# Seven products for eight in all large projections of a two-layer decoder trunk, with the middle of the layer in another order

## The chip, the core and the metric

One Trainium2 chip, and one of its cores. The engines of the core that matter here: TensorE (PE), which multiplies matrices into PSUM; VectorE (DVE) and ScalarE (ACT), which work on tiles of 128 partitions; SyncE (SP), whose queue issues the loads. The metric is the time of one execution on the device in microseconds (us).

## What is computed

Two layers over 256 tokens (S) of 2048 channels (D), all in float32:

```python
for i in range(DEPTH):
    h = rmsnorm(x, norm_mix_g[i])
    proj = h @ w_in[i]
    glu_in, q, k, v, f_logit, g_conv, g_attn = jnp.split(proj, split_pts, axis=-1)
    y_conv = conformer_conv(glu_in, ...)          # GLU, 31 taps, LayerNorm, swish, @ w_conv_out
    y_attn = forgetting_attention(q, k, v, log_f).reshape(...) @ w_attn_out[i]
    merged = sigmoid(g_conv) * y_conv + sigmoid(g_attn) * y_attn
    x = x + merged @ w_out[i]
    hf = rmsnorm(x, norm_ffn_g[i])
    gate, up = jnp.split(hf @ w_gate_up[i], 2, axis=-1)
    x = x + (silu(gate) * up) @ w_down[i]
    hp = rmsnorm(x, norm_ple_g[i])
    x = x + sigmoid(hp @ w_ple_gate[i]) * (p[i] @ w_ple_proj[i])
return rmsnorm(x, final_g)
```

There are 8 heads of 128 channels, 1024 channels of convolution, 5632 hidden channels in the feed-forward part and 256 channels of the embeddings p.

## The kernel before, in words

**Weights.** Every weight is streamed from HBM once, in tiles `raw` of 128x1024 float32 (two k-tiles of 128 rows by 512 columns), in a pool of seven. ACT rounds a tile to `wh` (line 140) and DVE subtracts to get the remainder `wl` (line 141); there are four buffers of each. The activations are split in the same way into xh and xl. A product of a k-tile is then three matmuls of 128x512: xh by wh, xh by wl, xl by wh (lines 175 to 177, in `Sum.add`). With two row blocks of tokens, one split tile `raw` feeds 12 matmuls.

**Two ways to make an output.** `chunk` makes 512 columns for all 256 tokens in the plain way, in groups of four k-tiles. `fast_chunks` makes two chunks of 512 columns together: of the first four k-tiles, taken as two halves of K, with the two chunks as the other dimension, it forms the eight block products with seven, as in Strassen's method in Winograd's form. That takes 42 matmuls for 48, sums of weight tiles on DVE (line 241 with `raw` and `sum`), a copy on ACT (line 254) and sums of the results `u` on DVE (lines 241, 255, 256, 271, 272), and an operand `Fast`, whose eight parts come from four subtractions (line 320) and two splits (lines 329, 330). The other k-tiles of the pair (`left`) are plain. Before the change, only the gate and up products of the feed-forward part, all but the first chunk, are made so: ten pairs in a layer.

**Stages of a layer.** Input projection: two GLU pairs of chunks, values, keys and queries; then four chunks of the convolution's gate (GATE_A) and four of the attention's gate (GATE_B). wA and wC take the attention's and the convolution's outputs, wOut their sum; then gate and up (wGU) and down (wD) in three parts of 3, 4 and 4 hidden chunks; then the embeddings' product (wPP) and their gate (wPG).

**Order.** `turns`, `tasks` and `background` are queues of deferred work. `run` (after each group of four k-tiles) does one deferred turn, such as the transposes of a finished chunk (line 295), or one task of the attention: the scores of a head, the transposes of its probabilities (lines 673 to 675), or its product with v. `fill` gives the background a credit of 7 after each group: convolution taps on DVE (line 490), then the steps of the LayerNorm. A tile framework then orders the queue of each engine by the dependences and the pools; each engine runs its own queue in order.

**Norms.** `Norm.squares` sums the squares of a finished chunk of x on ACT (line 368), `turn` transposes it on PE and splits it (lines 285, 286), or, for the first chunk of a fast norm, copies it into a `Fast` (line 314). The factor 1/rms is applied later, to the products. `residual` adds an output to x (line 822).

Of the attention's softmax, line 658 masks, 663 takes the maximum, 664 is the exponential, 665 and 666 scale. Lines 725 and 731 belong to the LayerNorm. Lines 878 to 881 are the sigmoid of the embeddings' gate, its product and the addition to x.

## Time and profile before

| what | us |
|---|---|
| three runs | 2891.22, 2891.67, 2892.88 |
| the profiled execution | 2891.74 |
| its span in the trace | 2889.9 |
| DMA, mean over the span | 188 GB/s, 54% of the 16 engines' time |

The profile lists for each engine the time in which it was busy; for each group of instructions the line of the kernel, the engine, output and input, the count, the busy time, the mean of one, and the idle time of the engine just before them with what ended it. A row of the timeline gives start, length, engine, line, operation and, in brackets, how long the engine had been idle and for whom. Rows that follow each other closely stand as one row with a count (x2). A row of windows gives for a stretch the busy time and the count of PE, of its weight loads (PEld), of DVE, ACT and POOL, then the granted clock of TensorE, the DMA share and GB/s. Tiles of one kind are told without their numbers there.

### The profile page before, as it was taken

To read this page: it belongs to the slowest core of one execution; us is meant where nothing else is said; L and a number is where in the kernel's file an instruction comes from. 1 tells how busy PE (TensorE), PEld (TensorE's weight loads), DVE (VectorE), ACT (ScalarE), POOL (GpSimd) and SP (SyncE) were. 2 spreads that over 40 slices of the span, in tenths; PEclk is the share of its full clock that TensorE was granted. 3 is DMA by queue.
4 is the path that set the end of the run, shared out by engine and by line. 5 is a ranking of instruction groups with operands and counts; after the bars stand their busy time and mean duration, and the time that the engine had idled before them with its cause. 6 is when DMAs were issued, how large, how long until landed. Compare 5 with 4: busy or idle time off the path is not lost.

```text
span 2889.9 us, 34305 instructions
## 1 busy us (share of the span) xinstructions
PE 2855.0 (99%) x12884; PEld 2361.8 (82%) x12884; DVE 2001.4 (69%) x2568; ACT 1431.1 (50%) x1726; POOL 9.5 (0%) x40
## 2 busy tenths in 40 slices
PE   8999999999999999999999999999999999999998
PEld 6888888788888888888888888887888888888886
DVE  5997745557678758865569966455585886688554
ACT  5445744455445435545554456444454554455444
POOL 0000000000000000000000000000000000000000
PEclk9999999999999999999999999999999999999999
DMA  7554455455556556555555544554455555556553
GB/s 279 180 179 166 166 197 191 165 185 180 207 183 209 198 178 211 182 204 189 183 176 188 180 163 175 195 190 162 177 191 207 182 196 204 181 197 211 186 203 122
DMA packets 149496, 543.27 MB, mean 188 GB/s; under 512 B 16849, under 2 KB 17105, under 8 KB 149073
## 3 DMA queue, kind: packets, MB, share of 16 engines
q1 hardware_dynamic: 149328, 541.07, 54.1%
q8 instruction: 101, 1.65, 0.2%
q14 instruction: 67, 0.54, 0.1%
HBM read 538.91 MB, written 2.10 MB: 187 GB/s over the span
## 4 chain that ended last, share of the span: by engine, by line
PE 94%; DVE 4%; DMA 1%; ACT 0%; issue 0%; SPq 0%; POOL 0%; ACTq 0%; POOLq 0%; DVEq 0%
PE mm L176 29%; PE mm L177 29%; PE mm L175 29%; PE ms L295 2%; DVE wl L141 2%; DVE pair L490 2%; PE ms L177 2%; PE ms L176 2%; PE ms L175 2%; DMA xt<-in_xR_dram 0%; PE ms L649 0%; DMA raw<-in_wI_dram 0%; PE ms L685 0%; ACT tmp L368 0%; PE ms L651 0%
## 5 line engine op out<-in xcount | busy, mean ns | idle before, releaser
L141 DVE TENSOR_TENSOR wl<-raw,wh 128x1024 fp32r<-128x1024 f32 x1054 | 1282.3, 1223 | 802.1 <-ACT wh L140 793.8
L140 ACT ACTIVATE wh<-raw 128x1024 fp32r<-128x1024 f32 x1054 | 1116.3, 1060 | 1299.9 <-PE mm L177 1186.1
L175 PE MATMUL mm<-wh,pair 128*128 128x512 f32 x3832 | 1502.8, 392 | 18.6 <-ACT wh L140 11.1
L176 PE MATMUL mm<-wl,pair 128*128 128x512 f32 x3832 | 1495.7, 390 | 1.8 <-DVE wl L141 1.8
L177 PE MATMUL mm<-wh,pair 128*128 128x512 f32 x3832 | 1495.9, 390 | 0.0
L175 PEld LDWEIGHTS mm<-wh,pair 128*128 128x128 f32 x3832 | 721.1, 188 | 166.9 <-ACT wh L140 12.0
L176 PEld LDWEIGHTS mm<-wl,pair 128*128 128x128 f32 x3832 | 721.8, 188 | 151.7 <-DVE wl L141 3.4
L177 PEld LDWEIGHTS mm<-wh,pair 128*128 128x128 f32 x3832 | 721.4, 188 | 150.7
L490 DVE SCALAR_TENSOR_TENSOR pair<-pair,vecs,pair 128x256 f32<-128x256 f32 x480 | 201.3, 476 | 0.0
L177 PE MATMUL ms<-wh,pair 128*128 128x512 f32 x192 | 74.7, 389 | 0.0
L175 PE MATMUL ms<-wh,pair 128*128 128x512 f32 x192 | 74.7, 389 | 0.0
L176 PE MATMUL ms<-wl,pair 128*128 128x512 f32 x192 | 74.7, 389 | 0.0
L241 DVE TENSOR_TENSOR raw<-raw,raw 128x1024 f32<-128x1024 f32 x60 | 73.2, 1221 | 0.9
L283 DVE TENSOR_TENSOR pair<-ms,pair 128x512 fp32r<-128x512 f32 (+1 forms) x76 | 45.1, 625 | 1.6 <-ACT pair L282 1.3
L822 DVE TENSOR_TENSOR xt<-xt,mm 128x512 f32<-128x512 f32 x64 | 41.1, 680 | 4.9 <-PE mm L177 4.9
L175 PEld LDWEIGHTS ms<-wh,pair 128*128 128x128 f32 x192 | 36.0, 188 | 7.5
L176 PEld LDWEIGHTS ms<-wl,pair 128*128 128x128 f32 x192 | 36.0, 188 | 7.5
L177 PEld LDWEIGHTS ms<-wh,pair 128*128 128x128 f32 x192 | 36.0, 188 | 7.5
L368 ACT ACTIVATE tmp<-xt 128x512 f32<-128x512 f32 x56 | 34.6, 619 | 14.9 <-DVE xt L822 8.8
L282 ACT ACTIVATE pair<-ms 128x512 fp32r<-128x512 f32 (+1 forms) x76 | 38.0, 541 | 0.6 <-PE ms L686 0.6
L285 ACT ACTIVATE pair<-ms,vecs 128x256 fp32r<-128x256 f32 x72 | 30.6, 467 | 14.4 <-DVE pair L286 14.4
L140 ACT ACTIVATE wh<-sum 128x1024 fp32r<-128x1024 f32 x20 | 21.2, 1062 | 31.3 <-PE mm L177 31.3
(167 smaller groups left out, 925.3 us busy)
## 6 DMA issues: line engine op xcount, KB each, us to landing
raw<-in_wGU_dram SPq DMA_DIRECT2D x352, 512.0 KB, 4.1
raw<-in_wI_dram SPq DMA_DIRECT2D x287, 512.0 KB, 3.8
raw<-in_wD_dram SPq DMA_DIRECT2D x176, 512.0 KB, 3.7
raw<-in_wOut_dram SPq DMA_DIRECT2D x64, 512.0 KB, 3.7
raw<-in_wPG_dram SPq DMA_DIRECT2D x64, 512.0 KB, 3.6
raw<-in_wA_dram SPq DMA_DIRECT2D x32, 512.0 KB, 4.2
raw<-in_wC_dram SPq DMA_DIRECT2D x32, 512.0 KB, 4.3
raw<-in_wPP_dram SPq DMA_DIRECT2D x8, 512.0 KB, 3.2
```

Of the source, the lines that this page charges most:

```text
L140: act.activation(h, raw, AF.Copy)
L141: dve.tensor_tensor(l, raw, h.bitcast(F32), op=ALU.subtract)
L175: pe.matmul(self.t, lhsT=xh, rhs=wh, start=start, stop=False)
L176: pe.matmul(self.t, lhsT=xh, rhs=wl, start=False, stop=False)
L177: pe.matmul(self.t, lhsT=xl, rhs=wh, start=False, stop=self.left == 0)
L241: add = lambda o, a, b: dve.tensor_tensor(o, a, b, op=ALU.add)
L282: act.activation(hi, src, AF.Copy)
L283: dve.tensor_tensor(lo, src, hi.bitcast(F32), op=ALU.subtract)
L295: pe.transpose(pt[:, kk * S + b * P : kk * S + (b + 1) * P], src(b)[:, c : c + P], ident)
L368: act.activation(tmp(), xt[:, b, n * 512 : (n + 1) * 512], AF.Square, accum_out=self.ss[:, b * 4 + n : b * 4 + n + 1],)
L490: dve.scalar_tensor_tensor(cv[c], u[c][:, j : j + S], w, cv[c], op0=ALU.mult, op1=ALU.add,)
L822: dve.tensor_tensor(xc, xc, acc[b], op=ALU.add)
```

## The change

Seven products for eight are now used in the two gates, in the output projection, in the embeddings' gate, and in the down projection (three parts of two pairs), as well as in gate and up as before: 28 pairs more in the two layers. Norms and merged values of these stages have a `Fast` operand; that of the very first norm is made from the transposed input (`early`); that of the down projection from the first hidden chunk of its part. The buffers of a `Fast` come from another pool. `fast_chunks` hands over its first chunk as soon as that is done (`first`).

The middle of a layer has another order. Before: four GATE_A chunks, with the second half of the attention and of the LayerNorm's work beneath them; then GATE_B and wA in turns; then four wC. Now: two GATE_B pairs, then the rest of the attention's tasks, four wA; then a GATE_A pair and two wC, twice. The credit of `fill` is split into 3 and 4 for each half group. The embeddings' products of two chunks are made ahead of a wPG pair, and ACT copies them out of PSUM (line 932 of the changed kernel).

```diff
-    def fast_chunks(fast, w1, w2, xs, ks):
+    def fast_chunks(fast, w1, w2, xs, ks, first, to=None):
...
-        def go(n=1):
+        def go(n=1, quiet=False):
...
-                    if len(left) % 2 == 0:
+                    fill(CONV // 2 + len(left) % 2)
+                    if not quiet:
                         run()
-                        fill(CONV)
...
-        u1, u3, u4, u5 = (tmp() for _ in range(4))
+        u1, u4, u3, u5 = [tmp() for _ in range(4)] if to is None else to
...
         add(u4, u4, c12.t)
+        first((u1, u4))
         go(2 * len(ks))
...
-        return (u1, u4), (u3, u5)
+        return u3, u5
...
-            self.f = [raws.tile([P, 4, 2, P], F32, tag="raw", name=f"fast{next(uid)}") for _ in range(2)]
+            self.f = [pair().rearrange("p a (n k s) -> p (a n) k s", n=2, k=2) for _ in range(2)]
...
+    def early():
+        norm.fast = Fast()
+        for j in range(2):
+            norm.fast.take(
+                j, xin[0][:, j, :].rearrange("p (k s) -> p k s", k=2), [norm.gain(2 * j + kk) for kk in range(2)]
+            )
+        norm.xs.update(enumerate(norm.fast.column_tiles()))
...
+                turns.append(early)
...
+            gate(fast_chunks(
+                norm.fast, wI[i, c], wI[i, c + 1], norm.xs, (4, 8, 12), gate,
+                [t[m][:, b, :] for m in range(2) for b in range(2)],
+            ))
...
-        for n in range(N4):
-            gate_a.append(sigmoids(GATE_A + n))
+        y_att = sigmoids(GATE_B) + sigmoids(GATE_B + 2)
         while tasks:
             run()
-        for n in range(N4 - 1):
-            t = sigmoids(GATE_B + n)
-            gated_by(t, attended(n))
-            y_att.append(t)
...
+        for n in range(N4):
+            gated_by(y_att[n], chunk(by_four(wA[i, n], 2), o_att, bank_mm))
...
+        fast_merged = Fast()
         for n in range(N4):
-            t = gate_a[n]
+            if n % 2 == 0:
+                gate_a = sigmoids(GATE_A + n)
+            if n == 0:
+                while background:
+                    fill(9)
+            t = gate_a[n % 2]
             gated_by(t, chunk(by_four(wC[i, n], 2), o_conv, bank_mm))
...
-        for n in range(N4):
-            residual(n, chunk(by_four(wOut[i, n]), merged, bank_mm))
-            advance(norm, n)
+        for n in range(0, N4, 2):
+            onto_x(norm, n + 1)(
+                fast_chunks(fast_merged, wOut[i, n], wOut[i, n + 1], merged, (4, 8, 12), onto_x(norm, n))
+            )
...
-            for n in range(N4):
-                groups = [(wD[i, n, c], range(4 * c, 4 * c + 4)) for c in range(c0, c0 + nch)]
-                residual(n, chunk(groups, hid, bank_mm))
+            for n in range(0, N4, 2):
+                await_x(hid, (4 * c0,))
+                on = after if part == len(FFN_PARTS) - 1 else None
+                onto_x(on, n + 1)(
+                    fast_chunks(
+                        fast_hid, wD[i, n][c0 : c0 + nch], wD[i, n + 1][c0 : c0 + nch], hid,
+                        range(4 * c0 + 4, 4 * c0 + 4 * nch, 4), onto_x(on, n),
+                    )
+                )
...
-            e = embed(n)
-            acc = chunk(by_four(wPG[i, n]), norm.xs, bank_mm)
+        for n in range(0, N4, 2):
+            for m in range(2):
+                e.append(pair())
+                for b, t in enumerate(chunk([(wPP[i, n + m], range(2))], ps, bank_ms)):
+                    act.activation(e[n + m][:, b, :], t, AF.Copy)
+            embedded(n + 1)(
+                fast_chunks(norm.fast, wPG[i, n], wPG[i, n + 1], norm.xs, (4, 8, 12), embedded(n))
+            )
```

In all, matmuls of 128x512 go from 12072 to 11904, DVE's 128x1024 from 1158 to 1378 and its 128x512 from 324 to 548 (two-operand operations), ACT's 128x1024 from 1080 to 1188. The DMAs stay 1037 on SP. The rows below show three places in the queues of the engines; in the changed kernel the lines have moved: 368 is now 383, 314 is 319, 329 is 334, 285 is 287, 241 is 242, 658 is 683, 663 is 688, 665 and 666 are 690 and 691, 725 and 731 are 750 and 756, 715 and 717 are 740 and 742, 673 to 675 are 698 to 700, 878 is 914.

**The first place: ACT, output projection of layer 0**, where the first chunk of x is finished and its norm begins. Before:

```order
L140 ACTIVATE wh815_4491<-raw814_4489 128x1024
L140 ACTIVATE wh818_4497<-raw817_4495 128x1024
L140 ACTIVATE wh823_4533<-raw822_4531 128x1024
L140 ACTIVATE wh826_4539<-raw825_4537 128x1024
L368 ACTIVATE tmp820_4527,small789_4362<-xt_82 128x512
L368 ACTIVATE tmp821_4529,small789_4362<-xt_82 128x512
L314 ACTIVATE fast787_4360<-ms830_4569,vecs_83 128x2x128 x2
L314 ACTIVATE fast787_4360<-ms831_4576,vecs_83 128x2x128 x2
L329 ACTIVATE pair832_4587<-fast787_4360 128x1024
L329 ACTIVATE pair834_4591<-fast788_4361 128x1024
L140 ACTIVATE wh837_4597<-raw836_4595 128x1024
L140 ACTIVATE wh840_4603<-raw839_4601 128x1024
```

Now:

```order
L140 ACTIVATE wh907_4765<-raw906_4763 128x1024
L140 ACTIVATE wh910_4783<-raw909_4781 128x1024
L140 ACTIVATE wh913_4801<-raw912_4799 128x1024
L383 ACTIVATE tmp894_4714,small841_4486<-xt_82 128x512
L383 ACTIVATE tmp895_4716,small841_4486<-xt_82 128x512
L140 ACTIVATE wh916_4819<-raw915_4817 128x1024
L319 ACTIVATE pair839_4484<-ms900_4737,vecs_83 128x2x128 x2
L319 ACTIVATE pair839_4484<-ms901_4744,vecs_83 128x2x128 x2
L334 ACTIVATE pair902_4755<-pair839_4484 128x1024
L140 ACTIVATE wh919_4837<-raw918_4835 128x1024
L334 ACTIVATE pair904_4759<-pair840_4485 128x1024
L140 ACTIVATE wh928_4870<-raw923_4861 128x1024
```

Four splits of weights stood ahead of the squares (L368) before, with none between the squares and the copies of the transposed x (L314), and the next split, wh837, behind the copies and both splits of the `Fast`. Now the next three (wh907, wh910, wh913) stand ahead of the squares (L383) and wh916 ahead of the copies (L319).

**The second place: DVE, attention of layer 0 beneath a gate.** Before, one of the later heads, tmp435 and tmp438, with GATE_A and the LayerNorm's centering (L725, L731):

```order
L658 SCALAR_TENSOR_TENSOR tmp435_2550<-ms434_2547,ct145_879,cmask_102 128x128
L663 TENSOR_REDUCE small436_2552<-tmp435_2550 128x1
L141 TENSOR_TENSOR wl461_2647<-raw459_2644,wh460_2646 128x1024
L665 RECIPROCAL small436_2552<-small436_2552 128x1
L658 SCALAR_TENSOR_TENSOR tmp438_2561<-ms437_2557,ct145_879,cmask_102 128x256
L666 TENSOR_SCALAR tmp435_2550<-tmp435_2550,small436_2552 128x128
L663 TENSOR_REDUCE small439_2563<-tmp438_2561 128x1
L725 SCALAR_TENSOR_TENSOR pair89_538<-ms440_2568,pair89_538 128x256 x2
L665 RECIPROCAL small439_2563<-small439_2563 128x1
L725 SCALAR_TENSOR_TENSOR pair89_538<-ms440_2568,pair89_538 128x256
L666 TENSOR_SCALAR tmp438_2561<-tmp438_2561,small439_2563 128x256
L731 TENSOR_TENSOR lsum441_2569<-lsum441_2569,tmp442_2574 128x256
```

Now, the head with tmp431 and tmp434, under the first GATE_B pair, from the second mask (L683) on; ahead of it stand two sums of 128x512 (L242), the first mask, the split wl459 and the first maximum:

```order
L683 SCALAR_TENSOR_TENSOR tmp434_2491<-ms433_2487,ct151_897,cmask_102 128x256
L740 TENSOR_TENSOR tmp440_2524<-pair95_556 128x256
L688 TENSOR_REDUCE small435_2493<-tmp434_2491 128x1
L742 TENSOR_TENSOR tmp440_2524<-tmp440_2524,pair95_556 128x256
L242 TENSOR_TENSOR sum481_2701<-raw477_2693,raw478_2695 128x1024
L690 RECIPROCAL small432_2482<-small432_2482 128x1
L742 TENSOR_TENSOR tmp440_2524<-tmp440_2524,pair95_556 128x256
L691 TENSOR_SCALAR tmp431_2480<-tmp431_2480,small432_2482 128x128
L690 RECIPROCAL small435_2493<-small435_2493 128x1
L742 TENSOR_TENSOR tmp440_2524<-tmp440_2524,pair161_943 128x256
L691 TENSOR_SCALAR tmp434_2491<-tmp434_2491,small435_2493 128x256
```

and a later head, tmp516 and tmp519, from the row behind its second mask on, up to the split wl531 that stands behind it:

```order
L756 TENSOR_TENSOR lsum494_2747<-lsum494_2747,tmp526_2894 128x256
L688 TENSOR_REDUCE small520_2860<-tmp519_2858 128x1
L750 SCALAR_TENSOR_TENSOR pair161_943<-ms493_2746,pair161_943 128x256
L242 TENSOR_TENSOR raw480_2699<-raw480_2699,raw477_2693 128x1024
L690 RECIPROCAL small517_2849<-small517_2849 128x1
L690 RECIPROCAL small520_2860<-small520_2860 128x1
L750 SCALAR_TENSOR_TENSOR pair161_943<-ms493_2746,pair161_943 128x256
L691 TENSOR_SCALAR tmp516_2847<-tmp516_2847,small517_2849 128x128
L691 TENSOR_SCALAR tmp519_2858<-tmp519_2858,small520_2860 128x256
L756 TENSOR_TENSOR lsum494_2747<-lsum494_2747,tmp527_2898 128x256
L750 SCALAR_TENSOR_TENSOR pair161_943<-ms493_2746,pair161_943 128x256
L141 TENSOR_TENSOR wl531_2909<-raw480_2699,wh530_2908 128x1024
```

Between the scores of such a head and its transposes PE has 48 matmuls of 128x512 in the first of the three cases, and 21 matmuls in the other two (in the last, two of these are small); in the last, PE's next matmul but one behind the transposes reads wl531. What moved: sums of weight tiles (L242, 128x1024) and the LayerNorm's steps (L740, L742, L750, L756) now stand between the mask and the scaling of a head.

**The third place: ACT, between the two pairs of the embeddings' gate in layer 0.** Before, between the first and the second chunk:

```order
L140 ACTIVATE wh2081_10802<-raw2080_10800 128x1024
L878 ACTIVATE tmp2064_10742<-mm2044_10608,rt2027_10553 128x512
L878 ACTIVATE tmp2065_10746<-mm2045_10612,rt2027_10553 128x512
L140 ACTIVATE wh2086_10834<-raw2085_10832 128x1024
L368 ACTIVATE tmp2066_10750,small2028_10555<-xt_82 128x512
L368 ACTIVATE tmp2067_10752,small2028_10555<-xt_82 128x512
L285 ACTIVATE pair2074_10779<-ms2073_10774,vecs_83 128x256
L140 ACTIVATE wh2089_10840<-raw2088_10838 128x1024
L285 ACTIVATE pair2074_10779<-ms2073_10774,vecs_83 128x256
L285 ACTIVATE pair2076_10789<-ms2075_10784,vecs_83 128x256
L140 ACTIVATE wh2092_10870<-raw2091_10868 128x1024
L285 ACTIVATE pair2076_10789<-ms2075_10784,vecs_83 128x256
```

Now, between the first and the second pair:

```order
L914 ACTIVATE tmp2257_11086<-tmp2257_11086,rt2213_10937 128x512
L914 ACTIVATE tmp2258_11087<-tmp2258_11087,rt2213_10937 128x512
L140 ACTIVATE wh2338_11475<-raw2337_11473 128x1024
L383 ACTIVATE tmp2308_11370,small2216_10941<-xt_82 128x512
L383 ACTIVATE tmp2309_11372,small2216_10941<-xt_82 128x512
L287 ACTIVATE pair2317_11400<-ms2316_11395,vecs_83 128x256
L287 ACTIVATE pair2319_11410<-ms2318_11405,vecs_83 128x256
L932 ACTIVATE pair2310_11374<-ms2314_11381 128x512
L932 ACTIVATE pair2310_11374<-ms2315_11385 128x512
L287 ACTIVATE pair2317_11400<-ms2316_11395,vecs_83 128x256
L287 ACTIVATE pair2319_11410<-ms2318_11405,vecs_83 128x256
L932 ACTIVATE pair2320_11417<-ms2324_11424 128x512
```

The copies of the embeddings' products (L932) are new, and stand behind the sigmoids (L914), the squares (L383) and the copies of the transposed x (L287); the fourth embeddings' product on PE is written to the banks that the first two copies read. Before, the embeddings' products stayed in PSUM until DVE took them (L879).

More of the change, by code (lines that the diff above doesn't have):

```diff
@@ L346, in column_tiles, with both, operand @@
                 )
-    def operand(xs, k0, src):
+        def both(self):
+            for k in range(4):
+                j, kk = divmod(k, 2)
+                yield self.h[0][:, 2 * j : 2 * j + 2, kk, :], self.l[0][:, 2 * j : 2 * j + 2, kk, :]
+    def operand(xs, k0, src, fast=None):
         for half, pt in turned(src):
+            if fast is not None:
+                fast.take(half, pt)
+                continue
             o = pair(F32R)
@@ L353, in operand @@
                 xs[k0 + 2 * half + kk] = by_blocks(o[:, kk, :])
+        if fast is not None:
+            xs.update(zip(range(k0, k0 + 4), fast.column_tiles()))
     class Norm:
@@ L824, in trunk, with onto_x, go @@
         norm = Norm(g_ffn, fast=True)
-        for n in range(N4):
-            residual(n, chunk(by_four(wOut[i, n]), merged, bank_mm))
-            advance(norm, n)
-        after = Norm(g_ple)
+        def onto_x(norm, n):
+            def go(y):
+                residual(n, y)
+                if norm is not None:
+                    advance(norm, n)
+            return go
+        for n in range(0, N4, 2):
+            onto_x(norm, n + 1)(
+                fast_chunks(fast_merged, wOut[i, n], wOut[i, n + 1], merged, (4, 8, 12), onto_x(norm, n))
+            )
+        after = Norm(g_ple, fast=True)
         c0 = 0
@@ L833, in trunk, with gate @@
             hid = {}
+            fast_hid = Fast()
             for c in range(c0, c0 + nch):
                 w1, w2 = wGU[i, 2 * c], wGU[i, 2 * c + 1]
+                z = [tmp() for _ in range(2)]
+                def gate(g, z=z):
+                    for b in range(2):
+                        act.activation(z[b], g[b], AF.Sigmoid, scale=norm.r(b))
+                        dve.scalar_tensor_tensor(z[b], g[b], norm.r(b), z[b], op0=ALU.mult, op1=ALU.mult)
                 if c == 0:
-                    g, t = [chunk(by_four(w), norm.xs, bank_mm) for w in (w1, w2)]
@@ L838, in trunk @@
-                    o = [tmp() for _ in range(2)]
-                else:
-                    g, t = fast_chunks(norm.fast, w1, w2, norm.xs, (4, 8, 12))
-                    o = t
+                    gate(chunk(by_four(w1), norm.xs, bank_mm))
+                    up = chunk(by_four(w2), norm.xs, bank_mm)
+                else:
+                    up = fast_chunks(norm.fast, w1, w2, norm.xs, (4, 8, 12), gate)
                 for b in range(2):
-                    z = tmp()
-                    act.activation(z, g[b], AF.Sigmoid, scale=norm.r(b))
-                    dve.scalar_tensor_tensor(z, g[b], norm.r(b), z, op0=ALU.mult, op1=ALU.mult)
-                    dve.scalar_tensor_tensor(o[b], t[b], norm.r(b), z, op0=ALU.mult, op1=ALU.mult)
@@ L863, in trunk @@
         last = i == L - 1
-        def embed(n):
-            return chunk([(wPP[i, n], range(2))], ps, bank_ms)
         if last:
```

97 lines of the change are left out of this document (46 added, 51 removed).

## The prediction

> **What bounds the kernel now.** I read the page first, for busy shares and the chain, then the waits of TensorE.
>
> ```profile
> PE 2855.0 (99%) x12884; PEld 2361.8 (82%) x12884; DVE 2001.4 (69%) x2568; ACT 1431.1 (50%) x1726; POOL 9.5 (0%) x40
> PE 94%; DVE 4%; DMA 1%; ACT 0%; issue 0%; SPq 0%; POOL 0%; ACTq 0%; POOLq 0%; DVEq 0%
> ...
> PE mm L175 <- ACT wh L140: 11.1, 3, 4.4
> PE mm L175 <- ACT wh L159: 7.5, 2, 6.8
> PE mm L176 <- DVE wl L141: 1.8, 3, 0.8
> ```
>
> TensorE (PE) is busy for 99% of the span and is 94% of the chain that ends last. Its waits (total, times, longest) add up to some 20 us: 7.5 at the start, and under "ACT wh" 11.1 at three places, of which two, one in each layer, are 4.4 us long. So the kernel is bound by matmuls, and the first question is what one costs where they follow each other:
>
> ```profile
> 1199.64 0.39 PE L175 MATMUL mm<-wh,pair 128*128 128x512 f32 x1
> ...
> 1204.40 0.39 PE L175 MATMUL mm<-wh,pair 128*128 128x512 f32 x1
> ```
>
> These two starts lie 21 matmuls apart: 4.76 / 21 = **0.2267 us** each. The 0.39 of a row holds the overlap with its neighbours.
>
> The second question is how much room VectorE (DVE) has, because every product saved on PE is paid there:
>
> ```profile
> core 0: us, PE busy (x) PEld busy (x) DVE busy (x) ACT busy (x) POOL busy (x), PEclk, DMA share, GB/s
> 220.00:240.00 20.00, 20.00 (x99) 16.81 (x98) 20.00 (x44) 10.73 (x18) 0.00 (x0) 1.00 0.47 168
> 800.00:900.00 100.00, 100.00 (x447) 82.87 (x446) 79.42 (x80) 50.10 (x52) 0.00 (x0) 1.00 0.55 190
> 1100.00:1200.00 100.00, 100.00 (x451) 82.93 (x450) 81.77 (x86) 52.53 (x56) 0.00 (x0) 1.00 0.59 202
> ```
>
> From 800 and from 1100 the gate and up products run, which have the seven products already: DVE stands at 79 to 82% and PE at 100%. That mix therefore fits beneath PE. Where the convolution's taps run (220 to 240), DVE is full, 20.00 of 20.00, and PE still never waits.
>
> **The removed matmuls.** The order has 28 fast pairs more (14 in a layer), each with 42 matmuls where 48 stood: 128x512 matmuls fall from 12072 to 11904, by 168. 168 x 0.2267 = **-38.1 us**, in full wherever PE stays the bound. The small logits matmuls change by 8 and count as nothing. The Trainium skill ("TensorE: Matmul & The Clock Gate", section "Back-to-back issue gap") gives about 131 ns per matmul for a sustained stream with 512 columns; by it the 168 would be worth 22.0 us and the time 16 us more than forecast. The trace disagrees: 0.2267 in a stream without a gap, nearer to the 216 ns that the page keeps for a matmul alone.
>
> **What it costs on the others.**
>
> ```profile
> L141 DVE TENSOR_TENSOR wl<-raw,wh 128x1024 fp32r<-128x1024 f32 x1054 | 1282.3, 1223 | 802.1 <-ACT wh L140 793.8
> L241 DVE TENSOR_TENSOR raw<-raw,raw 128x1024 f32<-128x1024 f32 x60 | 73.2, 1221 | 0.9
> L822 DVE TENSOR_TENSOR xt<-xt,mm 128x512 f32<-128x512 f32 x64 | 41.1, 680 | 4.9 <-PE mm L177 4.9
> ```
>
> DVE gets 220 more 128x1024 (x 1.22 = 268 us), 224 more 128x512 (x 0.68 = 152) and 48 more 128x256, in all some 430 us: 2001 becomes about 2430 of 2856, 85%. A pair over all of K has 42.2 us of matmuls (186 x 0.2267) against 19 splits, 4 large sums and 12 small ones on DVE, 23 x 1.22 + 12 x 0.68 = 36.2. Hidden on the average, as in the rows from 800 and 1100; so I cost these at nothing and look for places where the order makes PE wait for one particular instruction. The tightest pair is that of the first down projection, with three k groups: 138 matmuls, 31.3 us, against 19 x 1.22 + 12 x 0.68 = 31.3. Instructions that follow each other overlap by some 0.06 us, so 29.5 is nearer; if the cover is gone, two pairs in each of two layers lose up to 2 us each.
>
> **The wait in the output projection goes.** Where the normalised x of the next stage is begun, ACT's rows in before run: squares (L368), which wait for the residual; copies (L314), which wait for PE's transposes; splits; and only then wh837, which PE needs straight behind those transposes.
>
> ```profile
> 551.23 1.37 DVE L822 TENSOR_TENSOR xt<-xt,mm 128x512 f32<-128x512 f32 x2 [2.44 <-PE mm L177]
> ...
> 551.96 0.63 ACT L368 ACTIVATE tmp<-xt 128x512 f32<-128x512 f32 x1 [4.42 <-DVE xt L822]
> ...
> 557.79 1.57 ACT L314 ACTIVATE fast<-ms,vecs 128x256 f32<-128x256 f32 x4 [4.44 <-PE ms L295]
> ...
> 561.49 1.99 ACT L140 ACTIVATE wh<-raw 128x1024 fp32r<-128x1024 f32 x2
> ...
> 562.58 0.73 PE L175 MATMUL mm<-wh,pair 128*128 128x512 f32 x2 [4.39 <-ACT wh L140]
> 560.00:580.00 20.00, 16.70 (x66) 13.44 (x67) 12.34 (x13) 10.60 (x11) 0.00 (x0) 0.91 0.74 244
> ```
>
> PE waits 4.39, and the granted clock of that window is 0.91. The full price is read from the spacing of the transposes, one burst to a chunk, in each layer:
>
> ```profile
> 534.51 1.03 PE L295 MATMUL ms<-ident,pair 128*128 128x128 f32 x8
> 557.16 1.04 PE L295 MATMUL ms<-ident,xt 128*128 128x128 f32 x8
> 586.83 0.93 PE L295 MATMUL ms<-ident,xt 128*128 128x128 f32 x7
> ...
> 1988.52 0.71 PE L295 MATMUL ms<-ident,xt 128*128 128x128 f32 x5
> 2019.28 0.93 PE L295 MATMUL ms<-ident,xt 128*128 128x128 f32 x7
> ```
>
> Without the wait a step is 22.65 (534.51 to 557.16); with it 29.67 and 30.76. That is 7.0 and 8.1, together 15.1, against 4.4 each of plain waiting. In the changed order wh907, wh910 and wh913 stand ahead of the squares and wh916 ahead of the copies: each feeds 12 matmuls (2.72 us), so PE has four such blocks, 10.9 us, in hand, where it had none. What is late next is the squares' own chain, which ends in operands of the gate products, a whole pair later. **-15.1 us** (from nothing, if the wait comes back in another form, to -15.1). I cost the shorter waits that I add below at their own length; at the ratio of this one (7.5 to 4.4) they would come to 1.7 times as much, which is in rival (2). The Trainium skill (same page, "Part 1: The HAM clock gate") has the clock halved after an idle window of about 3.4 us; the 4.39 with a clock of 0.91 agrees, and by it waits of 1 to 3 us would cost their length and no more.
>
> **What the new order adds.** *Attention and conv norm, now under the gate pairs.* Here the pair's instructions stand between a head's scores and its softmax on DVE. In before:
>
> ```profile
> 238.62 0.28 PE L656 MATMUL ms<-chs,nsel 128*128 128x256 f32 x1
> ...
> 242.23 0.35 DVE L666 TENSOR_SCALAR tmp<-tmp,small 128x256 f32<-128x256 f32 x1
> ...
> L725 DVE SCALAR_TENSOR_TENSOR pair<-ms,pair 128x256 f32<-128x256 f32 x16 | 6.3, 413 | 0.0
> L663 DVE TENSOR_REDUCE small<-tmp 128x1 f32<-128x256 f32 x16 | 6.5, 409 | 0.2
> ```
>
> From the end of the last score to the end of the last product the softmax took 3.7 us there (238.90 to 242.58). After the change 21 matmuls (4.76 us) stand between the scores of the head with tmp431 and its transposes, where one of the later heads in before (tmp435) had 48. DVE's rows from the mask of tmp434 to its last product are ten of 128x256 or less (about 0.47 + 5 x 0.41 + 0.28 + 0.35 + 2 x 0.16) and one large sum: 4.7 us, and 7.9 if the five rows before them (two u's, a mask, a split, a maximum: 3.2) are still undone when the scores end. So PE waits between 0 and 3.2; with DVE nearly full I take 1.7, and half a us for the next head, whose chain is the same with less ahead. At tmp516 the rows from the second mask to wl531 come to 5.7 us at the same overlap, plus up to 2.6 of rows ahead, and PE wants wl531 5.4 after the scores: 0.3 to 2.9, I take 2.1, and 0.7 for the product with v right behind. **+5 a layer, +10** (0 to 18).
>
> *Embeddings.* ACT now copies the embeddings' products out of PSUM (L932), and the second one needs the banks of the first. In the changed order of ACT these copies stand behind the sigmoids (L914), squares (L383) and copies of transposes (L287) that close the pair before.
>
> ```profile
> 2875.72 1.37 ACT L878 ACTIVATE tmp<-mm,rt 128x512 f32<-128x512 f32 x2 [9.14 <-PE mm L177]
> 2878.45 0.63 ACT L368 ACTIVATE tmp<-xt 128x512 f32<-128x512 f32 x1 [1.35 <-DVE xt L881]
> ...
> L368 ACT ACTIVATE tmp<-xt 128x512 f32<-128x512 f32 x56 | 34.6, 619 | 14.9 <-DVE xt L822 8.8 <-DVE xt L881 4.2 <-DMA xt<-in_xR_dram 1.9
> L285 ACT ACTIVATE pair<-ms,vecs 128x256 fp32r<-128x256 f32 x72 | 30.6, 467 | 14.4 <-DVE pair L286 14.4
> L254 ACT ACTIVATE tmp<-ms 128x512 f32<-128x512 f32 x20 | 11.6, 582 | 0.0
> ```
>
> From sigmoid to squares is 2.73. Ahead of it a subtraction, 0.68; then two squares 1.24, two copies of transposes 0.93 and a copy out of PSUM like that of L254, 0.58: the bank is free 6.2 us after the pair's last matmul, and PE is there after 14 matmuls and 8 transposes (1.04, the row at 557.16), 4.2. I take 2.5, half a us above the difference for the second copy, for layer 0's second boundary and 1.0 for the first in each layer, which has no sigmoid; layer 1's second has no transposes ahead of the copies. **+4.5** (0 to 9).
>
> *Small.*
>
> ```profile
> 28.95 3.88 ACT L140 ACTIVATE wh<-raw 128x1024 fp32r<-128x1024 f32 x4
> 30.04 0.74 PE L175 MATMUL mm<-wh,pair 128*128 128x512 f32 x2 [2.35 <-ACT wh L140]
> ...
> L282 ACT ACTIVATE pair<-ms 128x512 fp32r<-128x512 f32 x60 | 32.0, 586 | 0.0
> L283 DVE TENSOR_TENSOR pair<-ms,pair 128x512 fp32r<-128x512 f32 x60 | 38.4, 681 | 0.0
> ```
>
> At 30 PE waits for a split that ACT begins when its squares are done; four copies for the new operand (1.57, the row of L314) now stand ahead of those: **+0.8** (0 to 3). The last hidden block of the first down projection is used 1.9 us after its transposes, for a copy and a subtraction of 1.27 together, with DVE's queue ahead: **+1.2** (0 to 4 for two layers). The last sigmoid waits for a subtraction of 0.68: **+0.7**. DMAs: as many and of the same size, in SP's queue in the order of the new products; their share is 0.47 to 0.59 in the windows above, so nothing.
>
> **Sum**: -38.1 - 15.1 + 10 + 4.5 + 0.8 + 1.2 + 0.7 = -36.0. The profiled execution took 2891.74 (span 2889.9 and 1.8 outside), the median of the runs is 2891.67: **2856 us**.
>
> **Rivals.** (1) *All new work is hidden*: DVE's backlog is shorter than I think, as from 220 to 240, where it was full and PE did not wait. 2891.7 - 38.1 - 15.1 + 2 = 2841. Against it: 4.76 us of cover for a chain of 4 or more. (2) *The waits grow*: DVE is the bound for stretches of the middle and of the first down projection, and waits above 4 us cost 7 to 8, as above. The three terms (10, 4.5, 1.2) at twice their size and 8 for the four tight pairs give 2856 + 15.7 + 8 = 2880. For it: 85% as a mean leaves little after a full stretch. (3) *The output projection's wait stays* in another place, since the squares and copies still wait for the same residual: 2856 + 15 = 2871. Against it: four splits in hand. (4) *Slower*: all softmaxes under the gate pairs come late. Five heads a layer, ten in all; if each makes PE wait for the whole chain of some 4 us, at the 7.5 that such a wait costs here, 75 stands in place of 10 and the time is 2921; it decides from 4.6 us a head, (36.0 + 10) / 10. Against it: DVE would have to be a whole head behind at each. (5) *The change does not cut the matmuls*: the order shows them cut; no chance of its own.
>
> **Chances.** Forecast 0.60, (1) 0.15, (2) 0.13, (3) 0.08, (4) 0.04. The range goes from (1), 2841, to 2876, short of (2), takes in (3) and the one-sided bounds of each term alone, and leaves out some 2 in 10: most of (2), (4) and the outer half of (1). About 0.2% (5.8 us) is what a measurement tells from no change: faster below 2885.9 0.93, within 0.04 (the upper end of (2), the lower of (4)), slower 0.03.
>
> **What would show it.** Right: PE's busy time down by about 38, no wait of 4.4 us, and no clock below 1, at the output projection; DVE near 2430; new waits of PE of 1 to 3 us for the softmax (L691) or wl in the middle, and for L932. Wrong: PE waiting in long runs for wl (L141) would say DVE is the bound; a clock under 1 in the middle would say the waits exceed what I gave them; PE busy down by less than 38 would say that the pitch is not what a removed matmul returns.

## The result, and the profile after

The changed kernel takes 2847.7 us (median of 4 runs, 2846.95 to 2848.3), the kernel before 2892.28 on the same chips (2891.22 to 2893.44): a ratio of 0.9846, with a 95% interval of 0.9829 to 0.9863. The profiled execution took 2847.62 us, its span 2845.8. That is 44.1 less than the profiled execution of before; the forecast was 36.

Of the changed kernel, first the page (busy time, and the chain that ended last), then the waits of PE (total, times, longest):

```profile
PE 2815.2 (99%) x12724; PEld 2328.0 (82%) x12724; DVE 2366.3 (83%) x3032; ACT 1556.2 (55%) x1874; POOL 9.5 (0%) x40
PE 92%; DVE 6%; ACT 1%; issue 1%; DMA 1%; SPq 0%; ACTq 0%; POOLq 0%; POOL 0%; DVEq 0%
```

```profile
PE mm L175 <- ACT wh L159: 7.5, 1, 7.5
PE mm L175 <- ACT wh L140: 4.9, 4, 3.1
PE ms L175 <- ACT pair L932: 2.1, 3, 1.1
PE mm L177 <- DVE pair L285: 0.8, 2, 0.4
PE mm L176 <- DVE wl L141: 0.4, 1, 0.4
```

PE is still the bound. DVE is busy for 365 us more and stands at 83%, and it appears in PE's waits with 1.2 us. The 3.1 is at the start; no wait of 4.4 is left. The output projection of layer 0, in ACT's timeline and as one window of the changed kernel (the columns are those of the windows of before):

```profile
551.36 1.06 ACT L140 ACTIVATE wh<-raw 128x1024 fp32r<-128x1024 f32 x1 [1.66 <-PE mm L177]
552.79 0.63 ACT L383 ACTIVATE tmp<-xt 128x512 f32<-128x512 f32 x1 [0.37 <-DVE xt L841]
...
554.13 1.06 ACT L140 ACTIVATE wh<-raw 128x1024 fp32r<-128x1024 f32 x1
555.11 1.18 ACT L319 ACTIVATE pair<-ms,vecs 128x256 f32<-128x256 f32 x3
```

```profile
525.00:612.00 87.00, 87.00 (x402) 72.42 (x401) 72.08 (x82) 52.29 (x68) 0.00 (x0) 1.00 0.61 205
```

A split stands ahead of the squares (L383) and one between them and the copies (L319). PE is busy for 87.00 of 87.00 us, at a granted clock of 1.00.

Every matmul of the weights' products is in both traces (12072 and 11904), so the time can be divided by stages: the time from the first matmul of a stage to that of the next, less 0.2267 for each matmul in it and the small matmuls' own. What is left in a stage is waiting or a slow clock. The first row is therefore count times spacing in both columns; the rows below it are what was measured, and the test of the first is that the sum comes out.

| term | forecast | measured |
|---|---|---|
| 168 matmuls | -38.1 | -38.1 |
| wait in the output projection, both layers | -15.1 | -15.1 |
| attention under the gates, both layers | +10 | +0.8 |
| embeddings' gate, both layers | +4.5 | +5.6 |
| first down projection, both layers | +1.2 | +1.4 |
| start | +0.8 | +0.4 |
| tail | +0.7 | +0.8 |
| sum | -36.0 | -44.2 |

The sum of the measured column, -44.2, meets the difference of the two executions, -44.1. One term was wrong: the attention. The start's 0.4 says little: what is lost to waiting and a slow clock in the first 42 us lies between 16.0 and 18.0 us in 13 of the 14 profiles of this document, whichever the kernel.

Between the pairs of the embeddings' gate, in layer 0, PE and ACT show the wait that was forecast:

```profile
1378.10 0.73 PE L175 MATMUL mm<-wh,pair 128*128 128x512 f32 x2 [1.20 <-ACT wh L140]
1380.86 0.50 PE L175 MATMUL ms<-wh,pair 128*128 128x512 f32 x1 [1.11 <-ACT pair L932]
...
1375.24 1.32 ACT L914 ACTIVATE tmp<-tmp,rt 128x512 f32<-128x512 f32 x2
...
1378.26 0.63 ACT L383 ACTIVATE tmp<-xt 128x512 f32<-128x512 f32 x1 [0.21 <-DVE xt L841]
...
1379.50 0.82 ACT L287 ACTIVATE pair<-ms,vecs 128x256 fp32r<-128x256 f32 x2
1380.22 1.08 ACT L932 ACTIVATE pair<-ms 128x512 f32<-128x512 f32 x2
```

PE's second wait ends when the first of the two copies (L932) is done, at some 1380.8, behind sigmoids, squares and copies of transposes. The first is for the split that stands behind the sigmoids (L914). By ACT's order it adds nothing to the whole: without it PE would stand longer for the banks, which are free 6.6 us after the pair's last matmul (it ends at 1374.19), where the forecast had 6.2.

And the two heads at which the forecast saw PE wait, in the timelines of DVE and PE:

```profile
282.01 0.28 PE L681 MATMUL ms<-chs,nsel 128*128 128x256 f32 x1
...
283.65 0.47 DVE L683 SCALAR_TENSOR_TENSOR tmp<-ms,ct,cmask 128x256 f32<-128x256 f32 x1
...
287.16 0.35 DVE L691 TENSOR_SCALAR tmp<-tmp,small 128x256 f32<-128x256 f32 x1
...
286.99 0.30 PE L698 MATMUL ms<-ident,tmp 128*128 128x128 f32 x1
287.60 0.30 PE L699 MATMUL ms<-ident,tmp 128*128 128x128 f32 x1
...
319.84 0.28 PE L681 MATMUL ms<-chs,nsel 128*128 128x256 f32 x1
...
320.28 0.48 DVE L683 SCALAR_TENSOR_TENSOR tmp<-ms,ct,cmask 128x256 f32<-128x256 f32 x1
...
324.48 1.22 DVE L141 TENSOR_TENSOR wl<-raw,wh 128x1024 fp32r<-128x1024 f32 x1
...
325.75 0.49 PE L176 MATMUL mm<-wl,pair 128*128 128x512 f32 x1
```

The last matmuls of the scores (L681) end at 282.29 and 320.12, and the second masks (L683) start at 283.65 and 320.28. The softmax of tmp434 ends at 287.51 and its transposes (L699) start at 287.60, two matmuls behind the transpose of tmp431 (L698); wl531 is done at 325.70 and read at 325.75. At tmp434 DVE is in time by 0.09 us, and at wl531 PE stands for less than 0.1.

### The profile page after: what moved, and what is told of

It reads as the page before. It is cut to its first block, busy times and chain, and to the rows that moved or that the text cites. A ratio compares the mean times of both kernels' runs of the same rounds, so it can differ in the third digit from the quotient of the medians.

```text
span 2845.8 us, 34651 instructions
## 1 busy us (share of the span) xinstructions
PE 2815.2 (99%) x12724; PEld 2328.0 (82%) x12724; DVE 2366.3 (83%) x3032; ACT 1556.2 (55%) x1874; POOL 9.5 (0%) x40
## 4 chain that ended last, share of the span: by engine, by line
PE 92%; DVE 6%; ACT 1%; issue 1%; DMA 1%; SPq 0%; ACTq 0%; POOLq 0%; POOL 0%; DVEq 0%
PE mm L177 27%; PE mm L176 26%; PE mm L175 26%; PE ms L175 3%; PE ms L177 3%; PE ms L176 3%; DVE wl L141 2%; DVE pair L514 2%; PE ms L297 2%; DMA pair<-in_xT_dram 0%; PE ms L674 0%; ACT wh L140 0%; DVE raw L242 0%; PE ms L710 0%; DMA raw<-in_wI_dram 0%
## 5 line engine op out<-in xcount | busy, mean ns | idle before, releaser
L140 ACT ACTIVATE wh<-raw 128x1024 fp32r<-128x1024 f32 x1110 | 1177.7, 1062 | 1126.2 <-PE mm L177 923.6
L141 DVE TENSOR_TENSOR wl<-raw,wh 128x1024 fp32r<-128x1024 f32 x1110 | 1345.7, 1223 | 424.6 <-ACT wh L140 410.8
L175 PE MATMUL mm<-wh,pair 128*128 128x512 f32 x3552 | 1392.5, 392 | 12.4 <-ACT wh L159 7.5
L176 PE MATMUL mm<-wl,pair 128*128 128x512 f32 x3552 | 1385.6, 390 | 0.5 <-DVE wl L141 0.4
L177 PE MATMUL mm<-wh,pair 128*128 128x512 f32 x3552 | 1385.2, 390 | 0.8 <-DVE pair L285 0.8
L175 PEld LDWEIGHTS mm<-wh,pair 128*128 128x128 f32 x3552 | 667.9, 188 | 148.9 <-ACT wh L159 7.5
L177 PEld LDWEIGHTS mm<-wh,pair 128*128 128x128 f32 x3552 | 667.6, 188 | 141.3 <-DVE pair L285 1.7
L242 DVE TENSOR_TENSOR raw<-raw,raw 128x1024 f32<-128x1024 f32 x144 | 175.9, 1221 | 1.8
L175 PE MATMUL ms<-wh,pair 128*128 128x512 f32 x416 | 162.9, 392 | 2.1 <-ACT pair L932 2.1
L177 PE MATMUL ms<-wh,pair 128*128 128x512 f32 x416 | 161.9, 389 | 0.0
L176 PE MATMUL ms<-wl,pair 128*128 128x512 f32 x416 | 161.9, 389 | 0.0
L175 PEld LDWEIGHTS ms<-wh,pair 128*128 128x128 f32 x416 | 78.1, 188 | 19.2 <-ACT pair L932 3.2
L177 PEld LDWEIGHTS ms<-wh,pair 128*128 128x128 f32 x416 | 78.1, 188 | 16.3
L140 ACT ACTIVATE wh<-sum 128x1024 fp32r<-128x1024 f32 x48 | 51.0, 1063 | 65.4 <-PE mm L177 65.4
L141 DVE TENSOR_TENSOR wl<-sum,wh 128x1024 fp32r<-128x1024 f32 x48 | 58.6, 1221 | 11.6 <-ACT wh L140 11.6
L242 DVE TENSOR_TENSOR sum<-raw,raw 128x1024 f32<-128x1024 f32 x48 | 58.6, 1221 | 1.5 <-DMA raw<-in_wGU_dram 0.9
L242 DVE TENSOR_TENSOR tmp<-tmp,mm 128x512 f32<-128x512 f32 x80 | 51.5, 681 | 0.0
L242 DVE TENSOR_TENSOR tmp<-tmp,ms 128x512 f32<-128x512 f32 x80 | 51.2, 681 | 0.0
```

Of the source, the lines that this page charges most:

```text
L140: act.activation(h, raw, AF.Copy)
L141: dve.tensor_tensor(l, raw, h.bitcast(F32), op=ALU.subtract)
L175: pe.matmul(self.t, lhsT=xh, rhs=wh, start=start, stop=False)
L176: pe.matmul(self.t, lhsT=xh, rhs=wl, start=False, stop=False)
L177: pe.matmul(self.t, lhsT=xl, rhs=wh, start=False, stop=self.left == 0)
L242: add = lambda o, a, b: dve.tensor_tensor(o, a, b, op=ALU.add)
```

## The experiments

The time of each is the median of four executions, and the ratio is to the kernel before, which ran beside it (medians of 2891.5 to 2892.2). Differences from the changed kernel are between series and hold to about 1 us. Where that matters, I use the traces: the time that PE's matmuls start later than at their usual spacing, added up behind the first 42 us, where the scatter of the start is left out.

### Where the wait in the output projection went

The prediction read from ACT's queue that the wait goes; it did not ask which of the edits puts the splits ahead. Two candidates: the seven products (theory Q) and the pool of the Fast operand's buffers (theory P).

**pool_alone**: the kernel before, with the pool edit only.

```diff
-            self.f = [raws.tile([P, 4, 2, P], F32, tag="raw", name=f"fast{next(uid)}") for _ in range(2)]
+            self.f = [pair().rearrange("p a (n k s) -> p (a n) k s", n=2, k=2) for _ in range(2)]
```

> The kernel before, with one edit: the two buffers of a Fast operand come from the pool of pairs (23) and no longer from the pool of raw weight tiles (7). Theory P (the pool edit alone removes the wait in the output projection, because the order of ACT's queue then has weight splits ahead of the squares and the copies): PE's two waits of 4.4 us go, with the half clock behind them, 7.0 and 8.1 us, so 2891.7 - 15.1 = 2877. Rival Q (the wait goes because the output projection is made with seven products): nothing changes, 2892. Rival R (fewer raw buffers were short of prefetch everywhere): more than 15 us goes.

Measured 2876.0, ratio 0.9944 (0.9930 to 0.9959): 15.7 less than before; behind the start the traces differ by 15.06. One line of code, and all of that term. **P** holds, Q falls, and so does R, since nothing is won elsewhere. PE's waits in it:

```profile
PE mm L175 <- ACT wh L159: 7.5, 1, 7.5
PE mm L175 <- ACT wh L140: 3.3, 1, 3.3
```

Only the start is left of the waits for ACT's splits.

**pool_undone**: the changed kernel without that edit (the diff above, the other way).

> The changed kernel, with the two buffers of every Fast operand back in the pool of raw weight tiles. Theory P: the wait in the output projection returns, 2847.6 + 15 = 2863 at least, and since five norms now begin with a Fast operand (two in front of gate and up, two in front of the embeddings' gate, one in front of the second layer) and not two, up to 5 x 7.5 = 37, so 2863 to 2885. Rival Q: no change, 2848.

Measured 2938.8, ratio 1.0162 (1.0145 to 1.0179): 91 more than the changed kernel, and slower than before. The direction is P's, the size two and a half to six times what I expected. Of pool_undone, one after the other: the page, PE's waits, SP's waits, a window, and ACT and PE in it, where the first hidden chunk of a part is turned into a Fast:

```profile
PE 2854.9 (97%) x12724; PEld 2347.5 (80%) x12724; DVE 2373.5 (81%) x3032; ACT 1552.8 (53%) x1874; POOL 9.5 (0%) x40
```

```profile
PE mm L175 <- ACT wh L140: 49.9, 17, 4.5
```

```profile
SPq L134 <- DVE pair L335: 131.7, 26, 12.1
```

```profile
680.00:700.00 20.00, 17.22 (x67) 13.25 (x66) 15.18 (x19) 10.28 (x11) 0.00 (x0) 0.83 0.63 202
```

```profile
683.95 1.09 ACT L316 ACTIVATE fast<-ms 128x512 f32<-128x512 f32 x2 [4.82 <-PE ms L297]
685.07 2.23 ACT L334 ACTIVATE pair<-fast 128x1024 fp32r<-128x1024 f32 x2
687.20 2.94 ACT L140 ACTIVATE wh<-raw 128x1024 fp32r<-128x1024 f32 x3
...
688.29 1.22 PE L175 MATMUL mm<-wh,pair 128*128 128x512 f32 x2 [2.56 <-ACT wh L140]
```

All 13 Fast operands that are made from something computed, not the norms' alone, now bring a wait: merged values, hidden chunks and norms. The expectation had counted five. ACT stands at the copies (L316) until PE has transposed, splits the Fast (L334), and only then splits weights. PE waits 51 us more than in the changed kernel (67 in the whole list against 16), and is busy for 40 us more with the same matmuls, since the clock is halved at the longer ones of these waits (0.83 in the window). 51 + 40 = 91.

SP's row tells why the splits stand behind: 26 loads wait for a Fast's split on DVE (L335), one for each of the two made of merged values and two for each of the other twelve, the very first norm's among them. In the kernel before there are four such waits (two operands; its row below), in pool_alone and in the changed kernel none:

```profile
SPq L134 <- DVE pair L330: 26.7, 4, 12.6
```

The next two weight loads are put into the buffers that the Fast gives back.

**pool_undone_nine**: is it the number of buffers? As pool_undone, with two more raw buffers.

```diff
-PAIRS = 23
-RAWS = 7
+PAIRS = 21
+RAWS = 9
```

> The changed kernel with the Fast buffers back in the pool of raw tiles, as in pool_undone, but with two more buffers in that pool (9, and 21 in the pool of pairs). Theory P1 (the load that follows the making of a Fast is put into a buffer that this Fast gives back, so it waits on SP's queue for the Fast's last split, whatever the number of buffers): as pool_undone, 2930 to 2945, and SP's waits for the Fast's split (L335) stay at 26. Rival P2 (seven raw buffers less two held ones are too few): 2848.

Measured 2943.4, ratio 1.0180 (1.0163 to 1.0197); SP waits 28 times for the Fast's split. The number is not the cause. P1 holds.

**before_splits_ahead**: the kernel before, pool untouched, with another order in the output projection.

```diff
-                parts = [split(fetch(src[:, o * 512 : (o + 2) * 512])) for o in range(0, len(ks), 2)]
+                parts = ready or splits(g)
+            ready = splits(g + 1) if ahead and g + 1 < len(groups) else None
...
-            residual(n, chunk(by_four(wOut[i, n]), merged, bank_mm))
+            residual(n, chunk(by_four(wOut[i, n]), merged, bank_mm, ahead=True))
```

> The kernel before, Fast buffers left in the pool of raw tiles, but in the output projection the loads and splits of the next four k-tiles are issued ahead of the deferred turn. Theory P1 (only what stands behind the Fast in ACT's and SP's queues counts): two splits, 24 matmuls or 5.4 us, now cover the copies and splits of the Fast, and the two waits of 4.4 us go: 2891.7 - 15.1 = 2877. Rival P2 (the shortage of raw buffers is the cause): 2885 to 2892.

Measured 2877.8, ratio 0.9952 (0.9937 to 0.9967): 13.8 less. SP still waits four times for the Fast's split, and PE does not wait there any more. So what counts is what PE has in hand while ACT stands at the copies; either edit gives it 24 matmuls or more.

**out_plain**: the changed kernel, output projection in plain chunks.

```diff
-        fast_merged = Fast()
...
-            turns.append(
-                lambda n=n, t=t: operand(merged, 4 * n, lambda b: t[:, b, :], fast_merged if n == 0 else None)
-            )
+            turns.append(lambda n=n, t=t: operand(merged, 4 * n, lambda b: t[:, b, :]))
...
-        for n in range(0, N4, 2):
-            onto_x(norm, n + 1)(
-                fast_chunks(fast_merged, wOut[i, n], wOut[i, n + 1], merged, (4, 8, 12), onto_x(norm, n))
-            )
+        for n in range(N4):
+            onto_x(norm, n)(chunk(by_four(wOut[i, n]), merged, bank_mm))
```

> The changed kernel with the output projection as plain chunks again (24 more matmuls of 128x512 in two layers). Theory P: 24 x 0.2267 = 5.4, so 2847.6 + 5.4 = 2853, and no wait of 4.4 us at the output projection. Rival Q: the wait returns too, 2853 + 15.1 = 2868.

Measured 2853.55, ratio 0.9866 (0.9852 to 0.9881): 5.9 more than the changed kernel, where 24 matmuls make 5.4; behind the start no other time is lost than there (21.56 and 21.55). Q falls a second time.

### Whether the middle costs anything

**gates_plain**: the changed kernel, both gates in plain chunks.

```diff
-            gate(fast_chunks(
-                norm.fast, wI[i, c], wI[i, c + 1], norm.xs, (4, 8, 12), gate,
-                [t[m][:, b, :] for m in range(2) for b in range(2)],
-            ))
+            for m in range(2):
+                pp = project(c + m)
+                for b in range(2):
+                    act.activation(t[m][:, b, :], pp[b], AF.Sigmoid, scale=norm.r(b))
```

> The changed kernel with both gates as plain chunks, in the new order of the middle (48 more matmuls in two layers). Theory M (the pairs under the attention cost at most 0.5 us, DVE is in time): 48 x 0.2267 = 10.9, so 2858.5. Rival N (the pairs cost the 10 us that I forecast, hidden by something else that I have not seen): 2848 to 2850.

Measured 2858.47, ratio 0.9884 (0.9869 to 0.9899): 10.8 more than the changed kernel, against 10.9 for 48 matmuls. The pairs in the middle pay in full; next to nothing of the forecast 10 is there.

**old_gate_order**: the changed kernel's pairs in the order of before.

```diff
-        y_att = sigmoids(GATE_B) + sigmoids(GATE_B + 2)
+        gate_a = sigmoids(GATE_A) + sigmoids(GATE_A + 2)
         while tasks:
             run()
-        for n in range(N4):
-            gated_by(y_att[n], chunk(by_four(wA[i, n], 2), o_att, bank_mm))
+        y_att = []
+        for n in range(0, N4, 2):
+            y_att += sigmoids(GATE_B + n)
+            for m in range(n, n + 2):
+                gated_by(y_att[m], chunk(by_four(wA[i, m], 2), o_att, bank_mm))
...
-            if n % 2 == 0:
-                gate_a = sigmoids(GATE_A + n)
...
-            t = gate_a[n % 2]
+            t = gate_a[n]
```

> The changed kernel with its pairs, but the gates in the order of before: both GATE_A pairs first, with the rest of the attention beneath them, then a GATE_B pair and two wA, twice, then four wC. Theory O (the new order of the middle brings nothing by itself): within 3 us of 2847.6, and no wait of PE over 1 us between the conv taps and the output projection. Rival S (the new order is what keeps the softmax and the LayerNorm in time): waits come up there, 5 to 15 us more.

Measured 2849.4, ratio 0.9853 (0.9835 to 0.9871): 1.7 more, within O's 3. In the traces the difference is in the start (17.7 and 16.6 lost there), and behind it both lose the same (21.4 and 21.55); no wait of PE in the middle is over 0.4. The reordering brings nothing that these runs can tell.

**sums_doubled** and **sums_fourfold**: how near is DVE to being the bound?

```diff
         add(s3, a11, a21)
+        add(s3, a11, a21)
```

> The changed kernel with one sum of weight tiles (128x1024 on DVE) done twice in each of the 48 fast pairs: 48 x 1.16 = 56 us more of DVE. Theory M (DVE is in time at most places, with some 6 us to spare in a pair over all of K, and nothing to spare at two places in a layer: the heads beneath GATE_B and the first down projection): 4 pairs of the first down projection and 4 pairs of GATE_B by 1.2 each, 5 to 10 us more, 2853 to 2858. Rival B (DVE is the bound as much as PE): most of 56, 2890 to 2904. Rival C (nothing is tight): 2848.

> The same sum four times: 48 x 3.5 = 167 us more of DVE, which makes its busy time some 89% of the span. Theory M: the eight tight pairs by 3.5 each, 28, and up to half as much again where waits bring the half clock: 2876 to 2890. Rival B: 2990 or more. Rival C: 2848.

Measured 2848.6 (ratio 0.9850, 0.9834 to 0.9866) and 2875.4 (0.9945, 0.9929 to 0.9961): 0.9 and 27.7 more, where DVE is busy for 51.6 and 158.2 us more. The doubled sum is hidden: rival C, and M was wrong there. But this does not show how tight the heads are, since the extra sum does not stand in their chain. The first head beneath GATE_B in sums_doubled, on DVE from its second mask on, and its transpose on PE:

```profile
284.26 0.47 DVE L684 SCALAR_TENSOR_TENSOR tmp<-ms,ct,cmask 128x256 f32<-128x256 f32 x1
...
287.76 0.35 DVE L692 TENSOR_SCALAR tmp<-tmp,small 128x256 f32<-128x256 f32 x1
...
288.36 1.22 DVE L242 TENSOR_TENSOR sum<-raw,raw 128x1024 f32<-128x1024 f32 x1
...
288.20 0.30 PE L700 MATMUL ms<-ident,tmp 128*128 128x128 f32 x1
```

The chain takes 3.86 us (284.26 to 288.12), as in the changed kernel, and the second sum comes behind it, at 288.36. The same holds in sums_fourfold. There the expected 167 us cost 27.7, as much as M said, but by luck, as most of it is not where M said. PE's row of the page and three of its waits behind the start in sums_fourfold:

```profile
PE 2827.1 (98%) x12724; PEld 2327.3 (81%) x12724; DVE 2524.5 (88%) x3176; ACT 1547.6 (54%) x1874; POOL 9.5 (0%) x40
```

```profile
PE ms L175 <- ACT wh L140: 5.3, 15, 0.5
PE ms L175 <- ACT pair L935: 4.9, 3, 1.9
PE mm L176 <- DVE wl L141: 4.5, 3, 2.0
```

There are 15 short waits for splits (L140), most at the starts of pairs, some waits at the embeddings, and one of 1.96 for wl (L141) in the second GATE_A pair of each layer; none is beneath GATE_B. B, DVE as a second bound, falls at this load: 27.7 of 167.

### Versions that go further

**embeddings_early**: the embeddings' products in the middle of the pair before.

```diff
+        def embeds(step, lo):
+            def go(y):
+                for m in range(lo, lo + 2):
+                    e.append(pair())
+                    for b, t in enumerate(chunk([(wPP[i, m], range(2))], ps, bank_ms)):
+                        act.activation(e[m][:, b, :], t, AF.Copy)
+                step(y)
+            return go
...
-                        range(4 * c0 + 4, 4 * c0 + 4 * nch, 4), onto_x(on, n),
+                        range(4 * c0 + 4, 4 * c0 + 4 * nch, 4), embeds(onto_x(on, n), 0) if on and n == 2 else onto_x(on, n),
...
-            for m in range(2):
-                e.append(pair())
-                for b, t in enumerate(chunk([(wPP[i, n + m], range(2))], ps, bank_ms)):
-                    act.activation(e[n + m][:, b, :], t, AF.Copy)
...
-                fast_chunks(norm.fast, wPG[i, n], wPG[i, n + 1], norm.xs, (4, 8, 12), embedded(n))
+                fast_chunks(norm.fast, wPG[i, n], wPG[i, n + 1], norm.xs, (4, 8, 12), embeds(embedded(n), 2) if n == 0 else embedded(n))
```

> The changed kernel with the embeddings' products and their copies out of PSUM in the middle of the pair before (the last pair of the down projection, and the first pair of the embeddings' gate), ahead of that pair's own sigmoids and squares, and no longer between two pairs. Theory E (the copies stand behind what closes a pair; the trace has 4.3 us of that in layer 0 and 1.4 in layer 1): 2847.6 - 5.6 = 2842. Rival: the copies or the products meet something else in the middle of the pair, and nothing is won, 2848.

Measured 2842.4, ratio 0.9829 (0.9813 to 0.9844): 5.3 less than the changed kernel, against 5.6 that the trace had; behind the start the traces differ by 5.7. PE's waits in it no longer name L932:

```profile
PE mm L175 <- ACT wh L159: 7.4, 1, 7.4
PE mm L175 <- ACT wh L140: 3.4, 1, 3.4
PE mm L177 <- DVE pair L285: 0.8, 2, 0.4
PE mm L176 <- DVE wl L141: 0.4, 1, 0.4
```

**early_and_first_pair**: that, and the first gate and up chunks as a pair.

```diff
                 if c == 0:
-                    gate(chunk(by_four(w1), norm.xs, bank_mm))
-                    up = chunk(by_four(w2), norm.xs, bank_mm)
-                else:
+                    await_x(norm.xs, (0,))
+                if True:
                     up = fast_chunks(norm.fast, w1, w2, norm.xs, (4, 8, 12), gate)
```

> embeddings_early, and the first gate and up chunks of each layer as a fast pair too (12 matmuls less in two layers). If matmuls bound that place as everywhere: 2842.4 - 12 x 0.2267 = 2839.6. Rival: the pair needs the Fast of the norm earlier than the plain chunk did, and waits for it: 2842 to 2850.

Measured 2838.9, ratio 0.9817 (0.9803 to 0.9832): 3.5 less than embeddings_early, against 2.7.

**start_splits_ahead**: that, and the splits ahead of the deferred turn in the very first chunk (the edit of before_splits_ahead, for that chunk).

> early_and_first_pair, and in the very first chunk the loads and splits of the next four k-tiles issued ahead of the deferred turn, so that ACT's eight squares of the first norm and the copies for its Fast no longer stand ahead of the splits that PE waits for. Theory T (that queue order is the wait at 26 us, 4.4 us there, and half clock behind it, 3.4 us more): 2838.9 - 4.4 - 3.4 = 2831. Rival (PE waits as long for the first split of the second chunk, or for the activations, which now load behind the weights): 2836 to 2840.

Measured 2836.2, ratio 0.9810 (0.9794 to 0.9827): 2.7 less, a third of what T expected and inside the rival's range. The first 40 us without this edit and with it:

```profile
0.00:40.00 40.00, 28.00 (x105) 21.85 (x106) 25.37 (x46) 29.74 (x55) 3.47 (x24) 0.91 0.90 336
```

```profile
0.00:40.00 40.00, 30.58 (x120) 24.05 (x121) 27.18 (x48) 30.76 (x56) 3.47 (x24) 1.00 0.88 337
```

The half clock is gone (0.91 to 1.00) and PE gets 15 matmuls further; 15 x 0.2267 = 3.4, which is also what the two spans differ by (2837.0 and 2833.6). T had counted too much in two places. The waiting did not go in full: two waits, 1.22 and 0.84, remain where the second chunk begins, in place of 4.36 and 0.35. And of the 6.83 us of half clock in the record of early_and_first_pair (27.75 to 34.57), 2.25 lay inside the wait, which ended at 30.00, so it cost 2.3 and not 3.4. Some 1 us of the rest is chance: at the program's start the clock is full from 10.68 us in one profile and from 12.62 in the other.

This last one is the fastest of all: 55 us under the kernel before.

## Why the prediction was right or wrong

- **-38.1 for 168 matmuls at 0.2267**: right, as far as the sum of the terms can tell (-44.2 against -44.1); out_plain and gates_plain returned 5.9 and 10.8 for 24 and 48, where the spacing makes 5.4 and 10.9.
- **-15.1 in the output projection**: right in size, from the spacing of the transposes, and right that splits ahead of the copies decide it (before_splits_ahead). It said nothing of the cause of that order. The pool of the Fast's buffers, an edit that the prediction priced nowhere, is the cause (pool_alone), and the changed kernel needs it far more than the kernel before: without it the seven products everywhere would have been 47 us slower than before (pool_undone). Rival (4) looked for the slower side in the softmaxes; it lay here.
- **+10 for the attention under the gates**: wrong, and the whole of the 8 us by which the forecast was too high; +0.8 is what the table finds. The step that failed is the two waits of PE for DVE, "I take 1.7" at tmp434 and "I take 2.1" at wl531, and it failed for a different reason at each. At tmp434 the 1.7 holds a queue of some 1.7 us ahead of the second mask, a chain of 4.7 and a cover of 4.76. The queue was not far off: 1.36 (the scores end at 282.29, the mask starts at 283.65). The chain took 3.86 (283.65 to 287.51): I had added mean durations, though instructions that follow each other on DVE overlap, by about 0.08 each here; I used such an overlap, with 0.06, at wl531 and not at tmp434. And the cover was 5.31, since the transposes that read tmp434 (L699, 287.60) stand two matmuls behind the one of tmp431, to which I had counted. At wl531 it was the queue: 0.16, where 2.1 holds 1.8; the chain took 5.42 for 5.7, and wl531 was wanted 5.63 after the scores for 5.4. That DVE comes just in time at both is luck as far as such a sum goes: none of its terms was known to 0.1 us.
- **Rival (1)**, that all new work is hidden (2841): its reason, a shorter backlog on DVE, was the right one at wl531. The measured 2847.7 lies between it and the forecast, as the waits of the embeddings and of the first down projection did come.
- **Embeddings +4.5, first down projection +1.2, start +0.8, tail +0.7**: right within about 1 us each (5.6, 1.4, 0.4, 0.8), and the first one shown by embeddings_early.
- **DVE**: 2366 us and 83% instead of 2430 and 85%, which is the same overlap: the durations of its instructions add up to 435 us more than before, its busy time to 365. That it stays hidden was right, and another 52 us of it stayed hidden too (sums_doubled).
- **The signs**: PE's busy time down by 39.8, a clock of 1.00 at the output projection and a wait for L932 came; the waits for the softmax (L691) and for wl in the middle did not.
- **Waits of 1 to 3 us at their own length**: right for those that came (1.20 and less, at a full clock), but not as a rule (last section). The prediction's sentence from the Trainium skill ("TensorE: Matmul & The Clock Gate", "Part 1: The HAM clock gate"), by which waits under some 3.4 us cost no clock, does not agree with these runs: all twelve waits of 2.56 us in pool_undone and pool_undone_nine did.

## What to carry to other kernels

A buffer that is held for long and given back late should not come from the pool that feeds the stream: the next loads are put into it, and with them the splits and matmuls behind fall back behind whatever frees it. Before a bound is called reached, ask at each place where an engine stands in its queue how many matmuls the busy engine has in hand; an order of instructions tells that without any time. Chains of short instructions on DVE are added by their starts, not by their durations.

## What the runs showed of the hardware that was not expected

How long a wait halves TensorE's clock: over the profiles of all these runs, the record of the granted clock has a stretch of half clock of 3.4 or 6.8 us at each of the 41 waits of 2.35 us and more (the wait for the first weights left out), and behind 2 of the 23 waits between 1.09 and 1.96 us. At half clock the matmuls follow each other every 0.43 us, so a wait costs up to 1.7 or 3.4 us more than its own length, and less where the stretch begins before the wait ends. In the kernel before, the stretches of 3.41 and 6.83 us, with two short waits for wl behind (0.72 and 0.24), bring the 4.39 us to 7.0 and 8.1. In pool_undone there are 13 such waits, of 2.56 to 4.51 us.
